# Odd-layer gates as float32r products one block later, and a new order of the routing work at the start of each expert stage

## The chip, the cores and the metric

One NeuronCore of a Trainium2 chip. The metric is device time in microseconds (us) of one execution; it is compared between kernels that run on the same chip. Engines are called PE (TensorE), DVE (VectorE), ACT (ScalarE), POOL (GpSimd) and SP (SyncE, which here only issues the weight loads).

## What is computed

Two residual layers over 512 tokens of width 1024, float32 in and out. Layer 0 has RWKV-7 time mixing and stick-breaking attention, and is not touched by the change. Layer 1 (the odd layer) is a gated recurrence, and both layers end with a mixture of experts. Cut to what matters:

```
# odd layer
u = rmsnorm(x) @ w_in_odd                       # 1024 -> 1280 gate branch | 1280 recurrent branch
rec = causal_depthwise_conv(u[..., 1280:])      # width 4
r = sigmoid(rec_g @ w_rgate[g] + b_rgate)       # 10 blocks g of 128 x 128
i = sigmoid(rec_g @ w_igate[g] + b_igate)
log_a = -8 * r * softplus(-lru_lambda)
h = scan(a = exp(log_a), b = sqrt(1 - a*a) * i * rec)
x = x + (gelu(u[..., :1280]) * h) @ w_out_odd
# every layer
g_idx = argmax(group softmax over 4 groups); top 2 of the group's 4 experts
gates = g_top * e_top / sum(e_top)
y = sum over chosen experts e of gates[e] * ((silu(h @ w_gate[e]) * (h @ w_up[e])) @ w_down[e])
```

## The kernel before, in words

**Precision.** A float32 matrix product is done as three float32r products: each operand is split into a high part (`hi`, an ACT copy that rounds) and a low part (`lo`, a subtraction on DVE or POOL), by `split` (L292), and hi\*hi + hi\*lo + lo\*hi are summed in PSUM. Only small products are left as plain fp32, among them the odd layer's gates (L1035, L1039).

**Order.** The program is written for a planner that orders each engine's instructions by its own cost estimates; `behind(a, b)` (L300) adds an order without a semaphore, so `a` comes after `b` in the planned order. Engines take their instructions in order. `switch` (L394) loads an activation table set and stands behind the activations that are listed for it.

**Odd layer** (`odd`, L994). A loop over 10 blocks g projects a recurrent block (`proj_fm`, L318: 24 products of 512 columns), scales it (L1021, DVE), convolves it (L1031 on ACT, three shifted L1033 on DVE) into `u[:, g]`, and right behind that makes the two gate products in fp32 (L1035, L1039), sigmoid, tanh and sigmoid on ACT (L1036, L1037, L1041), and u\*i on POOL (L1042). Then the table set is switched (L1044), and a second loop projects the 10 gate-branch blocks while decay, square root and scan of the recurrence run beside it (L1047 to L1064). `out_proj` closes the layer.

**Routing.** `route_tile` (L1150) is called per tile of 128 tokens inside `out_proj`. It writes the rows times the norm gain to `HD` in DRAM, from which expert rows are gathered; for the last tile that product is put off (`later`, L1159, on DVE) and called in `moe` as `last_rows` (L1463). `choose` (L1197) picks the experts of a tile. `place` (L1229) counts with triangular products on PE which slot a token has with each expert, and writes the slots (`pm`), the selection for expert 0 (`s0`, L1239) and a column of `rh`. `first` (L1243) forms expert 0's transposed rows with selection products on PE, without a gather.

**Expert stage** (`moe`, L1450). Each expert takes up to 96 tokens. First expert 0's x is split in 8 steps (`cut0`, L1462), then `route` (L1260) computes the gates and, through `slots` (L1308), the row numbers and factors of an expert: `match` (L1254, DVE) compares the slots with `io`, `rows_of` (L1324, PE) multiplies by `rh`, small DVE operations give the index. `fetch` gathers the next expert's rows with an indirect DMA on POOL (L1330). `half` (L1346) is the gate or the up product of an expert, 24 products; `front` the SiLU; `across` (L1334) turns gathered rows; `turn` and `down` are the second product of the expert before; `scatter` adds the result to DRAM. `chunk` (L1427) splits a weight chunk in two halves; for all experts but expert 0 the second halves of chunks 1, 3 and 5 go to POOL. For expert 0 the low parts stand behind `cut0`:

```
            pool = e > 0 and (i, j) in POOL
            if e == 0:
                self.behind(a, self.root)
                if not pool:
                    self.behind(v, self.cut0)
```

Weights come in 1 MB loads on SP's queue, in order, at most five under way (`load`, L1400), into a ring of buffers that `prefetch` (L1414) opens one by one as memory comes free.

## Time and profile before

| | us |
|---|---|
| median of 3 runs | 1229.35 (1228.08 to 1234.36) |
| the profiled execution | 1228.33 |
| its span, first to last instruction | 1226.6 |
| PE busy | 1160.2 |
| DVE busy | 986.5 |
| ACT busy | 807.0 |
| POOL busy | 483.7 |

The span runs through layer 0's mixing (to about 330), its experts (about 378 to 690), the odd layer (about 690 to 905) and its experts (about 910 to the end). How to read it: busy time is how long an engine held an instruction, and matmuls overlap, so PE's busy time is no measure of its speed; the distance between the starts of two matmuls is. The granted clock is the share of full speed (2.4 GHz) that PE had. A gap in brackets in a timeline is idle time of that engine ahead of the row, with what ended it.

### The profile page before, as it was taken

What the parts mean: (1) busy time and instruction counts of PE and PEld (TensorE: products, weight loads), DVE (VectorE), ACT (ScalarE), POOL (GpSimd) and SP (SyncE); (2) the same over time, 40 slices, a digit from 0 to 9 for tenths busy, and PEclk for the clock granted to TensorE, in tenths of its full rate; (3) what the DMA queues carried; (4) which work ended last, traced back from release to release, by engine and by line L of the source; (5) the groups of instructions that cost most, each with busy time, mean ns of one, the idle gap of its engine ahead of it and who ended that gap; (6) DMA issues with size and microseconds to landing.
All of it is one profiled execution on the core that took longest, in us unless ns stands there. A gap on an engine that the chain in (4) does not pass through costs nothing. (4 is left out here: it accounts for less than half of the span.)

```text
span 1226.6 us, 18324 instructions
## 1 busy us (share of the span) xinstructions
PE 1160.2 (95%) x6782; PEld 855.5 (70%) x6783; DVE 986.5 (80%) x1279; ACT 807.0 (66%) x1077; POOL 483.7 (39%) x319
## 2 busy tenths in 40 slices
PE   7999999899997899999999999999988999999997
PEld 6777776776675677777776766777766777777764
DVE  4387796577768799999998565697667999999986
ACT  6533545587536688888887564756436888888883
POOL 9043200210021367667765011300113566666753
PEclk9999999899998999999999999999998999999999
DMA  6312221016867899999993622276578999999974
GB/s 173 86 52 69 69 69 35 2 37 212 297 240 269 293 349 366 358 351 351 350 361 107 187 69 68 70 238 242 203 237 299 349 362 361 352 345 342 349 237 149
DMA packets 152390, 274.47 MB, mean 224 GB/s; under 512 B 8171, under 2 KB 59052, under 8 KB 152294
## 3 DMA queue, kind: packets, MB, share of 16 engines
q1 hardware_dynamic: 142438, 247.85, 58.5%
q0 software_dynamic: 7840, 18.04, 6.3%
q10 hardware_dynamic: 2016, 7.34, 1.5%
q8 instruction: 55, 0.90, 0.3%
q14 instruction: 41, 0.34, 0.1%
HBM read 258.80 MB, written 22.28 MB: 229 GB/s over the span
## 5 line engine op out<-in xcount | busy, mean ns | idle before, releaser
L297 ACT ACTIVATE R<-A 128x1024 fp32r<-128x1024 f32 (+1 forms) x451 | 473.1, 1053 | 193.1 <-PE ps_pj L1353 65.6
L298 DVE TENSOR_TENSOR R<-A,R 128x1024 fp32r<-128x1024 f32 (+1 forms) x362 | 494.1, 1398 | 82.8 <-ACT R L297 78.7
L298 POOL TENSOR_TENSOR R<-A,R 128x1024 fp32r<-128x1024 f32 x89 | 255.1, 2866 | 237.1 <-ACT R L297 232.8
L1354 PE MATMUL ps_pj<-R 128*96 128x512 f32 x512 | 205.6, 402 | 9.9 <-DVE R L298 9.9
L1352 PE MATMUL ps_pj<-R 128*96 128x512 f32 x512 | 206.2, 403 | 0.0
L1353 PE MATMUL ps_pj<-R 128*96 128x512 f32 x512 | 204.1, 399 | 0.0
L327 PE MATMUL ps_pj<-R 128*128 128x512 f32 x296 | 118.3, 400 | 3.5 <-DVE R L298 3.5
L325 PE MATMUL ps_pj<-R 128*128 128x512 f32 x296 | 119.4, 403 | 1.5 <-DVE A L700 0.6
L326 PE MATMUL ps_pj<-R 128*128 128x512 f32 x296 | 119.4, 403 | 0.0
L1354 PEld LDWEIGHTS ps_pj<-R 128*96 128x96 f32 x512 | 84.1, 164 | 47.0 <-DVE R L298 10.9
L1353 PEld LDWEIGHTS ps_pj<-R 128*96 128x96 f32 x512 | 84.4, 165 | 35.5 <-DVE R L298 0.3
L1379 PE MATMUL ps_at<-R 128*96 128x512 f32 x256 | 103.7, 407 | 5.0 <-PEq L1574 1.9
L1352 PEld LDWEIGHTS ps_pj<-R 128*96 128x96 f32 x512 | 84.5, 165 | 33.9 <-issue 0.5
L1381 PE MATMUL ps_at<-R 128*96 128x512 f32 x256 | 101.5, 396 | 0.0
L1380 PE MATMUL ps_at<-R 128*96 128x512 f32 x256 | 101.4, 396 | 0.0
L327 PEld LDWEIGHTS ps_pj<-R 128*128 128x128 f32 x296 | 55.6, 188 | 20.0 <-DVE R L298 5.7
L1388 POOL DMA_INDIRECT YD<-A x30 | 67.3, 2243 | 4.8 <-issue 2.4
L325 PEld LDWEIGHTS ps_pj<-R 128*128 128x128 f32 x296 | 55.6, 188 | 19.2 <-issue 3.4
L1155 POOL TENSOR_TENSOR A<-A 128x1024 f32<-128x1024 f32 x6 | 16.2, 2719 | 126.8 <-DVE A L861 87.2
L326 PEld LDWEIGHTS ps_pj<-R 128*128 128x128 f32 x296 | 55.6, 188 | 14.3 <-issue 3.6
L298 DVE TENSOR_TENSOR R<-ps_rw,R 128x384 fp32r<-128x384 f32 x92 | 47.7, 542 | 12.7 <-ACT R L297 12.6
L1257 DVE TENSOR_TENSOR A<-A 128x384 bf16<-128x384 f32 x32 | 57.8, 1817 | 0.0
(443 smaller groups left out, 1987.0 us busy)
## 6 DMA issues: line engine op xcount, KB each, us to landing
A<-in_exp_w_up_dram SPq DMA_DIRECT2D x61, 1024.0 KB
A<-in_exp_w_down_dram SPq DMA_DIRECT2D x61, 1024.0 KB
A<-in_exp_w_gate_dram SPq DMA_DIRECT2D x59, 1024.0 KB
A<-in_w_in_even_dram SPq DMA_DIRECT2D x27, 512.0 KB
A<-in_w_in_odd_dram SPq DMA_DIRECT2D x20, 512.0 KB
S<-in_exp_w_gate_dram SPq DMA_DIRECT2D x5, 1024.0 KB
A<-in_w_out_odd_dram SPq DMA_DIRECT2D x10, 512.0 KB
A<-in_x_dram SPq DMA_DIRECT2D x8, 512.0 KB
```

The costliest lines, as they stand in the source:

```text
L297: a = self.nc.scalar.activation(hi, src, AF.Copy)
L298: return a, (eng or self.nc.vector).tensor_tensor(lo, src, hi.bitcast(F32), OP.subtract)
L325: nc.tensor.matmul(p[0:n], hi[:, k], Hh[:, k], start=k == 0, stop=False)
L326: nc.tensor.matmul(p[0:n], hi[:, k], Hl[:, k], start=False, stop=False)
L327: nc.tensor.matmul(p[0:n], lo[:, k], Hh[:, k], start=False, stop=k == KD - 1)
L1352: self.nc.tensor.matmul(b, xh[:, k], hi, start=k == 0, stop=False)
L1353: self.nc.tensor.matmul(b, xl[:, k], hi, start=False, stop=False)
L1354: self.nc.tensor.matmul(b, xh[:, k], lo, start=False, stop=k == KD - 1)
L1379: nc.tensor.matmul(yb[n], hh[:, k], hi[:, cs], start=k == 0, stop=False)
L1380: nc.tensor.matmul(yb[n], hl[:, k], hi[:, cs], start=False, stop=False)
L1381: nc.tensor.matmul(yb[n], hh[:, k], lo[:, cs], start=False, stop=k == 3)
L1388: self.nc.gpsimd.indirect_dma_start(out=self.YD[l][:, :], out_offset=bass.IndirectOffsetOnAxis(ap=ix[0:SL], axis=0), in_=y.rearrange("p a ...
```

## The change

1. Odd layer: the two fp32 gate products of a block become three float32r products each. For that `u[:, g]` and the block's gate weights are split. The gates of block g - 1 are made after the projection of block g has closed (`gates`, `self.closed`), those of the last block after the first projection of the gate branch, and the switch of the table set moves there with them.
2. Expert stage: expert 0's chunk 0 is split ahead of the x splits, its low parts behind `chosen` and `placed` instead of `cut0`; the second halves of its chunks 3 and 5 go to POOL. The last tile's row product moves from DVE, behind the x splits, to POOL, once tiles 0 to 2 are placed. `route` first makes what expert 0's SiLU and expert 1's gather need; all that needs the gate values moves into a new function `gates`, called after expert 0's two halves, with the buffers, the load and expert 2's gather that follow from it. `match` reads `io` from a copy in PSUM. Copies of `rh` columns go from DVE to ACT. The count of overflow blocks takes 3 DVE operations instead of 10. Row products are held behind the last product of the half before (`closed`).

The diff, cut to its core:

```diff
@@ odd
+        def gates(g):
+            hi, lo = [self.uq.bufs[g % 2].r(T, off=i * T) for i in range(2)]
+            self.split(hi, lo, u[:, g])
+            wh, wl = [self.wq.r(2, 128, off=i * 256) for i in range(2)]
+            self.split(wh, wl, wgv[:, :, g])
+            z = []
+            for x in range(2):
+                z.append(self.bank("rw"))
+                for i, (a, b) in enumerate(((wh, hi), (wh, lo), (wl, hi))):
+                    m = nc.tensor.matmul(z[x], a[:, x], b, start=not i, stop=i == 2)
+                    if not x and not i:
+                        self.behind(m, self.closed)
...
         for g in range(NB):
             b = self.proj_fm(w, LRU + g * 128, 128, ("pj", "at")[g % 2])
...
-            nc.tensor.matmul(z, wgv[:, 0, g], u[:, g], start=True, stop=True)
...
-            nc.tensor.matmul(z, wgv[:, 1, g], u[:, g], start=True, stop=True)
...
+            if g:
+                gates(g - 1)
...
             scaled(mm[:, g], self.proj_fm(w, g * 128, 128, ("pj", "at")[g % 2]))
+            if not g:
+                gates(NB - 1)
+                self.switch(sig, "exp_and_others")
@@ route_tile
-            self.last_rows = later
...
         if t == NT - 1:
-            self.place(0, t)
+            m = nc.gpsimd.tensor_tensor(h.f(), self.X.f(NT, D)[:, t], self.gn.f(), OP.mult)
+            self.tc.add_manual_dep(m.ins, self.place(0, t).ins.name, mybir.DependencyInfo(
+                mybir.DependencyClass.Sync, mybir.DependencyReason.DATA), reason="order")
+            nc.gpsimd.dma_start(self.HD[t * 128:t * 128 + 128, :], h.f())
...
-            self.sel[0], self.p0 = self.sl.next().b(NT, SL), self.bank("rw")
-            self.match(0)
-            self.rows_of(self.p0[0:SL, 0:3], self.sel[0], self.rh.b(NT, NE, 9)[:, :, 0, 0:3])
@@ match
+        return self.nc.vector.tensor_tensor(self.sel[e], self.pi[:, 256:256 + SL].rearrange("p (a n) -> p a n", a=1).to_broadcast(s),
+                                            self.pm.f(NT, NE)[:, :, e:e + 1].to_broadcast(s), OP.is_equal)
@@ route
-        self.slots(0, 0, 1)
+        nc.scalar.activation(self.pi[:, 256:256 + SL], self.io.f()[:, 0:SL], AF.Copy)
...
-            V.tensor_copy(rh[:, :, :, c], bc(r, NE))
+            nc.scalar.activation(rh[:, :, :, c], bc(r, NE), AF.Copy)
...
+        self.slots(0, 2, 3)
+        self.slots(1, 0, 1)
...
+    def gates(self):
+        self.behind(V.tensor_reduce(gs, gd, AX.X, OP.add), self.lastlo)
...
-            V.tensor_copy(rh[:, :, :, c], ga)
+            nc.scalar.activation(rh[:, :, :, c], ga, AF.Copy)
...
-        self.slots(0, 1, 3)
+        self.slots(0, 0, 2)
+        self.slots(1, 1, 3)
@@ slots
+        self.rows_of(p[:, a * 3:b * 3], self.sel[e], self.rh.b(NT, NE, 9)[:, :, e, a * 3:b * 3], behind=self.closed)
@@ chunk
-            pool = e > 0 and (i, j) in POOL
+            pool = (i, j) in (POOL if e else POOL[1:])
...
-                    self.behind(v, self.cut0)
+                    self.behind(v, self.cut0 if i else self.placed if j else self.chosen)
@@ moe
+        part0 = self.chunk(l, 0, 0)
         for k in range(KD):
             self.cut0 = self.split(nxt[0][:, k], nxt[1][:, k], self.x0[k // 4][:, k % 4 * SL:k % 4 * SL + SL], g=self.gf(l, k))[1]
-        self.last_rows()
...
         self.route(l)
...
-        self.prefetch(l, 1, False)
...
             if e == 0:
-                self.slots(1)
                 fetch(1)
...
-            if e < NE - 2:
+            if 0 < e < NE - 2:
                 self.slots(e + 2)
                 fetch(e + 2)
...
             b = self.half(1, xh, xl, part)
             nc.vector.scalar_tensor_tensor(hd, b, r, hd, OP.mult, OP.mult)
+            if not e:
+                self.gates()
+                yr = Ring(ar, 2, D, *room)
+                self.prefetch(l, 1, False)
+                self.slots(2)
+                fetch(2)
             nxt = turned(e + 1)
```

## Rows read from the trace of the kernel before

**Rows 1.** Windows, steady expert loop: us, busy time (instructions) per engine, clock, DMA share, GB/s.
```profile
590.00:610.00 20.00, 20.00 (x99) 14.23 (x98) 19.94 (x22) 16.65 (x20) 15.54 (x6) 1.00 1.04 359
```

**Rows 2.** Windows, PE behind the first wait of layer 0's experts, columns as above.
```profile
383.50:389.20 5.70, 5.67 (x14) 3.80 (x15) 5.67 (x18) 2.33 (x3) 0.00 (x0) 0.51 0.90 323
```

**Rows 3.** Timeline of PE, start of layer 0's experts.
```profile
377.87 0.46 PE L1352 MATMUL ps_pj<-R 128*96 128x512 f32 x1
...
383.53 0.74 PE L1354 MATMUL ps_pj<-R 128*96 128x512 f32 x1 [4.98 <-DVE R L298]
...
402.00 0.85 PE L1341 MATMUL ps_rw<-A 96*128 96x96 f32 x8 [4.29 <-DMA A<-HD,A]
...
403.15 0.72 PE L1352 MATMUL ps_pj<-R 128*96 128x512 f32 x1
```

**Rows 4.** Timeline of DVE, the same stretch.
```profile
370.02 0.27 DVE L1241 TENSOR_SCALAR A<-A 128x48 bf16<-128x48 f32 x1
...
375.58 0.17 DVE L1237 SCALAR_TENSOR_TENSOR A<-ps_pj,A 128x16 f32<-128x16 f32 x1 [0.92 <-PE ps_pj L1235]
...
380.74 1.22 DVE L1160 TENSOR_TENSOR A<-A 128x1024 f32<-128x1024 f32 x1
```

**Rows 5.** Timeline of PE, start of layer 1's experts.
```profile
910.05 0.45 PE L1352 MATMUL ps_pj<-R 128*96 128x512 f32 x1
...
936.28 0.72 PE L1352 MATMUL ps_pj<-R 128*96 128x512 f32 x1
```

**Rows 6.** Timeline of PE, one block of the odd layer's first loop.
```profile
748.51 1.10 PE L1035 MATMUL ps_rw<-A 128*128 128x512 f32 x2 [0.36 <-DVE A L1033]
...
750.54 0.40 PE L326 MATMUL ps_pj<-R 128*128 128x512 f32 x1
...
755.80 0.39 PE L325 MATMUL ps_at<-R 128*128 128x512 f32 x1
```

**Rows 7.** Timeline of DVE in that loop.
```profile
751.21 0.69 DVE L1021 TENSOR_TENSOR A<-ps_pj,A 128x512 f32<-128x512 f32 x1 [2.84 <-PE ps_pj L327]
...
754.06 2.31 DVE L1033 SCALAR_TENSOR_TENSOR A<-A 128x511 f32<-128x511 f32 x3
...
768.48 3.35 DVE L1033 SCALAR_TENSOR_TENSOR A<-A 128x511 f32<-128x511 f32 x3
```

**Rows 8.** Windows, the odd layer's first loop and the stretch behind it.
```profile
710.50:782.70 72.20, 68.60 (x258) 47.40 (x258) 41.79 (x48) 36.64 (x50) 13.06 (x9) 1.00 0.23 67
785.50:842.00 56.50, 52.89 (x227) 41.86 (x226) 55.89 (x70) 39.41 (x60) 7.31 (x6) 1.00 0.58 190
```

**Rows 9.** Groups of instructions by line and form: busy us, mean ns, idle before.
```profile
L298 DVE TENSOR_TENSOR R<-A,R 128x1024 fp32r<-128x1024 f32 x356 | 488.0, 1404 | 79.7 <-ACT R L297 78.7 <-DMA A<-in_gn_w_dram 0.2
L298 POOL TENSOR_TENSOR R<-A,R 128x1024 fp32r<-128x1024 f32 x89 | 255.1, 2866 | 237.1 <-ACT R L297 232.8 <-DMA A<-in_exp_w_up_dram 3.9
...
L295 ACT ACTIVATE R<-ps_at,A 128x96 fp32r<-128x96 f32 x16 | 4.8, 338 | 4.0 <-PE ps_at L1252 2.6 <-DVE R L296 1.4
...
L830 ACT ACTIVATE R<-A 128x512 fp32r<-128x512 f32 x8 | 4.5, 619 | 0.0
...
L1291 DVE TENSOR_TENSOR A<-A 128x64 f32<-128x64 f32 x4 | 1.1, 277 | 0.1
```

**Rows 10.** All instructions of the match, L1257: duration ns min/median/max.
```profile
L1257 DVE TENSOR_TENSOR A<-A x32: 538/2682/2697, 376.0 to 1123.1; 128x384 bf16<-128x384 f32 x32
```

**Rows 11.** Timeline of POOL, the gather of expert 1 in layer 0.
```profile
394.11 1.19 POOL L1330 DMA_INDIRECT A<-HD,A  x1 [11.28 <-DVE A L1320]
```

**Rows 12.** DMA issues: out<-in, queue, count, KB, median us from issue to landing.
```profile
HD<-A POOLq DMA_DIRECT2D x2, 512.0 KB, 6.9
A<-HD,A POOLq DMA_INDIRECT x30, 7.7
```

**Rows 13.** Timeline of SP, issue of expert 15's gate weights in layer 0.
```profile
618.74 2.97 SPq L1406 DMA_DIRECT2D A<-in_exp_w_gate_dram  x2
```

**Rows 14.** Timeline of PE, first product of expert 15 in layer 0.
```profile
653.97 0.39 PE L1352 MATMUL ps_pj<-R 128*96 128x512 f32 x1
```

More of the change, by code (lines that the diff above doesn't have):

```diff
@@ L41 @@
 WO1 = LOW + 7056
+YR = 17352
 FLY = 5
@@ L1070, in odd @@
             scaled(mm[:, g], self.proj_fm(w, g * 128, 128, ("pj", "at")[g % 2]))
+            if not g:
+                gates(NB - 1)
+                self.switch(sig, "exp_and_others")
+                for x in (self.uq, self.wq):
+                    x.free()
             if g < 2:
@@ L1125, in route_begin @@
         lo = (MID, LOW)[l]
-        self.ss, self.rb, self.s0 = ar.get(16, lo), ar.get(504, lo), ar.get(NT * SL, lo)
+        end = (YR, 1 << 30)[l]
+        self.rb = ar.get(504, MID) if l else ar.take(end, 504)
+        self.ss, self.s0 = ar.get(16, lo, end), ar.get(NT * SL, lo, end)
         self.gn = ar.get(D, lo)
@@ L1281, in route @@
             self.after(nc.scalar.activation(a, a, AF.Exp))
-        V.tensor_reduce(gs, gd, AX.X, OP.add)
+        for b in (self.scr, self.ht, self.ss, self.s0, self.gn):
+            b.free()
+    def gates(self):
+        nc, ar, V, R = self.nc, self.ar, self.nc.vector, self.R
+        bc = lambda a, n: a.to_broadcast([128, NT, n])
+        OH, rh = self.OH.b(NT, NE), self.rh.b(NT, NE, 9)
+        gs, gd, ex, den, g1, EX, ga = [R[k] for k in ("gs", "gd", "ex", "den", "g1", "EX", "ga")]
+        self.behind(V.tensor_reduce(gs, gd, AX.X, OP.add), self.lastlo)
         V.tensor_scalar(den, ex, 1.0, None, OP.add)
@@ L1288, in route @@
         for c in range(3, 6):
[L1289 removed]
+            nc.scalar.activation(rh[:, :, :, c], ga, AF.Copy)
             if c < 5:
                 V.tensor_tensor(ga, ga, rh[:, :, :, c], OP.subtract)
[L1292 to L1294 removed]
+        self.slots(0, 0, 2)
+        self.slots(1, 1, 3)
+        nx, n = self.bank("rw"), (T - 1) // SL
         for t in range(NT):
[L1296 to L1301 removed]
+            m = nc.tensor.matmul(nx[:, 0:16], self.tri[:, 1], OH[:, t], start=t == 0, stop=t == NT - 1)
+            if not t:
+                self.behind(m, self.closed)
+        ex, s = R["n"].rearrange("p t n -> p (t n)"), [128, NE, n]
+        more = R["LG"].rearrange("p t n -> p (t n)")[:, 0:NE * n].rearrange("p (a n) -> p a n", a=NE)
+        V.tensor_tensor(more, nx[:, 0:16].rearrange("p (a n) -> p a n", n=1).to_broadcast(s),
+                        self.io.f()[:, SL - 1:n * SL:SL].rearrange("p (a n) -> p a n", a=1).to_broadcast(s), OP.is_gt)
+        V.tensor_reduce(ex[:, 0:16], more, AX.X, OP.add)
         V.tensor_reduce(ex[:, 16:17], ex[:, 0:16], AX.X, OP.add)
[L1303 removed]
+        self.ext = ar.get(24, 0, self.slots_at[0])
         V.tensor_copy(self.ext.i(17), ex[:, 0:17])
[L1305 removed]
+        for b in (self.rb, self.OH):
             b.free()
@@ L1310, in slots @@
         nc, V = self.nc, self.nc.vector
-        p = self.pi[0:SL, e * 9:e * 9 + 9] if e else self.p0[0:SL, 0:9]
+        p = self.pi[0:SL, e * 9:e * 9 + 9]
         sg = self.sg.f(NE, 3, p=(0, SL))[:, e]
-        if e:
+        if e not in self.sel:
             self.sel[e] = self.sl.next().b(NT, SL)
-            self.match(e)
-        if e or a:
-            self.rows_of(p[:, a * 3:b * 3], self.sel[e], self.rh.b(NT, NE, 9)[:, :, e, a * 3:b * 3])
+            m = self.match(e)
+            if e < 2:
+                self.behind(m, self.placed)
+        self.rows_of(p[:, a * 3:b * 3], self.sel[e], self.rh.b(NT, NE, 9)[:, :, e, a * 3:b * 3], behind=self.closed)
         V.tensor_reduce(sg[:, a:b], p.rearrange("p (c k) -> p c k", c=3)[:, a:b], AX.X, OP.add)
@@ L1322, in slots, with rows_of @@
                 V.tensor_scalar(self.lastt.f(p=(0, SL))[:, 0:1], sg[:, 0:1], self.slot.f()[0:SL, 0:1], 1.0, OP.add, OP.add)
-    def rows_of(self, out, sel, rh, t0=0, t1=NT):
-        for t in range(t0, t1):
-            self.nc.tensor.matmul(out, sel[:, t], rh[:, t], start=t == 0, stop=t == NT - 1)
+    def rows_of(self, out, sel, rh, behind=None):
+        for t in range(NT):
+            m = self.nc.tensor.matmul(out, sel[:, t], rh[:, t], start=t == 0, stop=t == NT - 1)
+            if behind and not t:
+                self.behind(m, behind)
     def gather(self, xg, ix):
@@ L1481, in moe @@
             if e == 0:
-                self.slots(1)
                 fetch(1)
-            part = lambda i, e=e: self.chunk(l, e, i)
+            part = lambda i, e=e: self.chunk(l, e, i) if e or i else part0
             hd = hr.next().f(p=(0, SL))
```

49 lines of the change are left out of this document (17 added, 32 removed).

## The prediction, written before the change was run

> **What bounds the kernel now.** I read the windows of the steady expert loop first [rows 1]: TensorE (PE), VectorE (DVE) and the DMA are all full there. PE decides, since a wait of PE would be listed, and in the loop none is. So time can be won only where PE's own timeline prints an idle gap or where its clock is down, and both stand where the change is made. At the start of layer 0's experts [rows 3] PE issues its first product at 377.87, soon waits 4.98 us for the lower half of a weight, then takes 5.7 us for 14 products (granted clock 0.51, the 1.2 GHz level [rows 2]), and after expert 0 waits 4.29 us for the gathered rows of expert 1. Layer 1 repeats it [rows 5]. In the odd layer [rows 6] the fp32 gate products come behind an idle 0.36 us; from 785 us on DVE is full, 55.9 of 56.5 us [rows 8].
>
> **Part A, the odd layer's gates.** From 710.5 us, where block 2's projection starts, to the end of the gate branch's first projection at 782.7 there are 72.2 us [rows 8]; they hold 9 projections and 10 gate groups. Projection products start 0.229 us apart (23 steps from 750.54 to 755.80 [rows 6]); a projection has 24: 5.49 us. So a gate group costs (72.2 - 49.4)/10 = 2.28 us, and a block 7.77. One group's parts agree: from its start 748.51 to 750.54, where the second projection product behind it starts, less 0.229 for the first one, is 1.8 [rows 6]; the rest is the gap ahead. After the change a group is six one-pass products of 0.229: 1.37 us, a block 6.86. Ceiling 10 x 0.91 = **9.1**.
>
> Added are four splits per block. Of u (512 columns): ScalarE (ACT) 0.62 [rows 9], DVE about 0.69, as its other 512-column operation [rows 7]. Of the gate weights (256 columns): not in the trace; between a 96-column and a 512-column row on ACT, 0.34 to 0.62 [rows 9], between 64 and 512 columns on DVE, 0.28 to 0.69; I take 0.4 each, nearer the small ones in size. DVE's 0.69 + 1.40 + 2.31 = 4.40 per block [rows 7, 9] becomes 5.5, under 6.86: DVE's idle time covers it, and ACT's does (36.6 us busy of 72.2 [rows 8], 10 more). Not surely covered is the chain: u is ready 5.16 us after its projection (751.21 to 754.06 + 2.31 [rows 7]); with split and hand-overs 6.5 us, while the gates come at 6.86. If POOL's product u*i falls on the three shifts, they take 3.35 instead of 2.31 [rows 7]: 7.5. A lateness is halved, as a whole block lies between: block (6.86 + 7.5)/2 = 7.18, 5.9 us won. With one weight split, the next weights' cut and the three gate activations all ahead of it I bound the chain at 10.5: block 8.68, 9.1 us lost. I take **-7.5**, midway between 9.1 and 5.9, as neither the free chain nor the stretched row is nearer.
>
> This arrives: the table switch waits for the last gates, which start at 710.5 + 49.4 + 9 x 1.37 = 772.2 instead of 780, and DVE, full from there to 842 [rows 8], starts that much sooner. What is late next is DVE in that stretch.
>
> **Part B, the start of the experts, in both layers.** From expert 0's first product to expert 1's: 403.15 - 377.87 = 25.3 us [rows 3], in layer 1 936.28 - 910.05 = 26.2 [rows 5]. In it are 48 products (11.0), the transposes of expert 1's rows (1.15, 402.00 to 403.15), the two waits (9.3), and 14 products at the low clock, 14 x (0.405 - 0.229) = 2.5 too long; 1.4 us are left for small row products. So 13.5 us of work: ceilings **11.8** and **12.7**.
> - *First wait.* DVE comes out of the x splits at 380.7 and does the last tile's row product first (1.22 [rows 4]), then the small gate operations among the weight splits. After the change chunk 0 is split while DVE waits for PE (0.92 us idle ahead of the last placing [rows 4], and during the last selection products), and the row product is on POOL. PE goes on from 377.9. Chunk 1 still stands behind the x splits, 380.7 + 1.2 = 381.9; PE is there at 381.1.
> - From there DVE has five weight splits (1.22 alone, as the row product of that size), about 1.4 us of small operations and two matches (0.54 [rows 10]): to 389.3; 10 of PE's products, 2.3 us, follow: 391.6 instead of 388.9. Loss 0 (small ones in gaps) to 2.7; I take 1.7, nearer the full count, DVE being in order. No gap is long, so the full clock is kept.
> - *Second wait.* The gather of expert 1 is issued at 394.11 [rows 11] and used from 402.0; 7.7 us to landing in the median [rows 12]. After: the row product on POOL from the placing of tiles 0 to 2 (370.3 [rows 4]) for 2.9 us, as POOL's other product of that size [rows 9], then the write, 6.9 [rows 12]: 380.1. Gather there, landed at 388; PE wants it at 390. Covered by some 2 us; without that cover PE waits what is missing, up to the old 4.3.
> - *The gates* now stand between expert 0 and 1: eight small DVE operations of at most 0.28 and three ACT copies of some 0.34 [rows 9], 3.3 us in a row beside PE's last 2.3. PE's row products queue behind them, and expert 1's transposes behind those if so planned: 0 to 2 us; I take 0.8, since only the excess of 1.0 is uncovered.
> - *At the front* splitting chunk 0 can delay the placing: 0 to 1.2; casts that leave DVE give back up to 0.28 each, as the 64-column row [rows 9]. I take 0.2.
>
> Per layer 2.7 of the ceiling is lost: **-9.1** and **-10.0**.
>
> **Costed at nothing.** ACT's copy of io and the casts: ACT waits for PE there. POOL's splits of expert 0 (2.87 each [rows 9]): the second gather stands behind the first of them, but has an expert's time to land. The load moved behind the gates, and every load queued behind it on SP: expert 15's gate weights are issued at 618.74 and used from 653.97, 35 us later [rows 13, 14]; this cover, less five transfers under way, goes if PE gains much more than 12 us. The shorter match (median 2.68 now [rows 10]) pays nothing: PE never waits for it in the loop.
>
> **Sum**, against the profiled execution: 1228.3 (span 1226.6 + 1.7) - 7.5 - 9.1 - 10.0 = 1201.7; the median shown is 1.0 above that execution. Forecast **1202**, own range 1194 to 1209.
>
> **Rivals.** About 0.5% (6 us) is what a measurement of this kernel can tell from no change.
> 1. *DVE paces expert 0.* Beside a POOL split DVE's two-input operations stretch (match 0.54 to 2.68 [rows 10]): five splits at the mean 1.40 instead of 1.22, one block of 2.1, and PE's gaps bring the low clock back (2.5): 5.5 us per layer, **1213**. For: DVE has little room there. Against: POOL takes only one split ahead of PE's last product. Chance 0.15. The Trainium skill, page "SBUF — State Buffer", section "Who interferes with whom", speaks for this rival: a DVE instruction with two SBUF inputs and a GpSimd instruction that reads SBUF exclude each other for a whole instruction. By it alone POOL's row product and two splits could hold DVE 3 x 2.9 us per layer, and the sum would be 1219; the spread of the match agrees with it. By the same rule a match that reads io from PSUM no longer waits.
> 2. *The gates wait in every block.* u ready at 8.3 us (shifts stretched, one ACT operation more): block 7.58, part A gives 1.9: **1207**. For: the 3.35 row; against: 5.16 in the old order. 0.09.
> 3. *It does not do what it says.* A stated order is only a lower bound: the planner can still put chunk 0 behind the x splits, and POOL's queue can hold the gather. Part B then gives 2 us per layer, part A little: **1222 to 1226**. 0.08.
> 4. *Slower.* The row products of expert e+2 are held behind the last product of expert e's gate half, in PE's queue. If the match, on the full DVE, is later than that, PE waits at 13 places per layer: at 2.1 us each 55 us, **1256**; slower than now by 0.5% from 1.3 us each on. For: DVE is full [rows 1]. Against: nothing in the loop waits now. 0.06.
>
> **Numbers.** Forecast 0.62, rivals 0.15, 0.09, 0.08, 0.06. Faster 0.86 (forecast, 1 and 2), same 0.08, slower 0.06. The range 1192 to 1217 takes in the bounds of the sum and rivals 1 and 2.
>
> **What would show it.** Right: gate groups of six products, 1.4 us; blocks of 6.9 to 7.2; the table switch 7 to 8 us earlier; no wait of 5 us behind expert 0's first products and no low clock there; the gather of expert 1 issued 2 to 4 us after expert 0's first product; expert 1 some 16 us behind expert 0. Wrong: an idle gap ahead of each gate group, a clock near 0.5 in expert 0, a wait for gathered rows, or PE waits in the loop.

## The result, and the profile of the changed kernel

The changed kernel takes 1218.44 us in the median (1213.68 to 1219.83, five runs), the kernel before 1229.26 (1228.08 to 1234.36, five runs): a ratio of 0.9896 (95% interval 0.9876 to 0.9915). It is faster, by 10.8 us (about 1%) instead of the 27 forecast, and lies above both ranges of the prediction, which end at 1209 and 1217. In one run each of `odd_alone` and `rows_last` below (1338.8 and 1628.2 us) the mean granted clock was only 0.81 and 0.65, and medians and ratios leave them out. The changed kernel's profiled execution took 1217.41 us with a span of 1215.7; the span before was 1226.6.

Where the 10.9 us between the two profiled spans lie, from PE's timelines:

| stretch | before | after | difference | forecast |
|---|---|---|---|---|
| start to expert 0's first product, layer 0 | 377.87 | 379.61 | +1.7 | 0 |
| from there to expert 2's first product, layer 0 | 44.13 | 40.86 | -3.3 | -9.1 |
| on to the odd layer's first projection | 272.66 | 272.73 | +0.1 | 0 |
| odd layer, first projection to first placing | 205.8 | 201.05 | -4.7 | -7.5 |
| on to expert 0's first product, layer 1 | 9.62 | 9.05 | -0.6 | 0 |
| from there to expert 2's first product, layer 1 | 44.70 | 41.53 | -3.2 | -10.0 |
| on to the end | 271.85 | 270.87 | -1.0 | 0 |

The first line is no cost of the change: in two executions of the same code up to that product it starts at 377.87 (before) and at 381.03 (the run `odd_alone` below).

**The expert stage.** PE's timeline at the start of layer 0's experts, where [rows 3] had waits of 4.98 and 4.29 us:

```profile
379.61 0.47 PE L1384 MATMUL ps_pj<-R 128*96 128x512 f32 x1
...
392.90 0.47 PE L1386 MATMUL ps_pj<-R 128*96 128x512 f32 x1 [1.19 <-POOL R L299]
...
396.79 1.54 PE L1373 MATMUL ps_rw<-A 96*128 96x96 f32 x8 [2.63 <-DMA A<-HD,A]
...
398.68 0.72 PE L1384 MATMUL ps_pj<-R 128*96 128x512 f32 x1
...
400.23 0.41 PE L1356 MATMUL ps_o<-A 128*96 128x6 bf16 x4 [0.82 <-ACT A L1315]
```

The first wait is gone. In its place PE waits for a split on POOL, for expert 1's gathered rows, and inside expert 1 for the copies of the gate values. Expert 1 starts 19.1 us behind expert 0 (forecast: 16). POOL's timeline says why:

```profile
375.07 0.57 POOL L1194 DMA_DIRECT2D HD<-A  x1 [0.30 <-POOL A L1191]
...
383.95 6.48 POOL L1362 DMA_INDIRECT A<-HD,A  x1 [8.30 <-DVE A L1294]
390.46 2.38 POOL L299 TENSOR_TENSOR R<-A,R 128x1024 fp32r<-128x1024 f32 x1
```

The gather holds POOL for 6.48 us, not for the 1.19 of [rows 11], and the split stands behind it. Its rows land at 396.75, 12.8 us after it is issued. On DVE the index (L1350) is ready only at 383.66, and then a train of five splits runs without a gap; the gather ends 1.0 us after that train:

```profile
383.45 0.21 DVE L1350 TENSOR_SCALAR A<-A 96x1 int32<-96x1 f32 x1
...
383.71 5.76 DVE L299 TENSOR_TENSOR R<-A,R 128x1024 fp32r<-128x1024 f32 x5
...
390.07 2.87 DVE L1313 TENSOR_TENSOR A<-A 128x64 f32<-128x64 f32 x1
```

The third row is one of the small gate operations (0.22 us in index_first below): beside POOL's late split, 390.46 to 392.84, it takes 2.87. So POOL waits for DVE in the gather, and DVE for POOL right behind it. The gather of [rows 11] had subtractions of the same kind beside it in the kernel before, but a small reduction of data in PSUM stood between two of them; the gather, issued at 394.11, ended at 395.30, beside the second subtraction:

```profile
394.31 0.16 DVE L1318 TENSOR_REDUCE A<-ps_o 96x3 f32<-96x9 f32 x1
394.39 1.22 DVE L298 TENSOR_TENSOR R<-A,R 128x1024 fp32r<-128x1024 f32 x1
```

Layer 1 repeats what the changed kernel does in layer 0 (gather 6.17 us, gate operation 3.09), and expert 2's rows come late there too:

```profile
903.30 0.47 PE L1384 MATMUL ps_pj<-R 128*96 128x512 f32 x1
...
921.97 0.72 PE L1384 MATMUL ps_pj<-R 128*96 128x512 f32 x1
...
938.60 0.85 PE L1373 MATMUL ps_rw<-A 96*128 96x96 f32 x8 [1.37 <-DMA A<-HD,A]
```

The windows (columns as in [rows 1]) show the clock behind the waits: 0.54, near the 1.2 GHz level, from expert 1's transposes on. It falls in the wait for the gathered rows (0.69 from 393.90 to 396.79) and is at 0.50 from its end on, ahead of the wait for the gate values; the second row shows that. The third row is the whole stretch from expert 0's first product to expert 2's.

```profile
396.80:406.00 9.20, 8.38 (x38) 6.22 (x39) 5.96 (x14) 4.04 (x8) 2.88 (x2) 0.54 0.56 196
...
396.79:398.68 1.89, 1.89 (x12) 1.89 (x13) 0.43 (x1) 0.80 (x2) 0.00 (x0) 0.50 1.03 342
...
379.61:420.47 40.86, 35.81 (x171) 24.35 (x169) 35.57 (x64) 28.44 (x44) 20.51 (x7) 0.87 0.89 316
```

The same stretch of the kernel before:

```profile
377.87:422.00 44.13, 34.87 (x161) 24.35 (x159) 36.38 (x74) 27.29 (x39) 9.43 (x6) 0.88 0.81 282
```

**The odd layer.** Blocks are 7.33 us long (752.57 to 759.90; from 737.56 on 7.31 to 7.58), against 7.46 to 8.01 before. PE issues a group's first product and then waits for the lower half of u:

```profile
752.57 0.39 PE L1035 MATMUL ps_rw<-S 128*128 128x512 f32 x1
753.19 1.43 PE L1035 MATMUL ps_rw<-S 128*128 128x512 f32 x5 [0.23 <-DVE S L299]
...
759.90 0.40 PE L1035 MATMUL ps_rw<-S 128*128 128x512 f32 x1
```

ACT's and DVE's timelines of that block hold the chain. ACT takes the sigmoid of the block before (L1038, which waits for PE's gate product) ahead of this block's convolution (L1052):

```profile
753.96 0.69 ACT L1038 ACTIVATE A<-ps_rw,A 128x512 f32<-128x512 f32 x1 [0.36 <-PE ps_rw L1035]
754.54 0.81 ACT L1052 ACTIVATE A<-A 128x512 f32<-128x512 f32 x1
...
759.11 0.63 ACT L298 ACTIVATE S<-A 128x512 fp32r<-128x512 f32 x1 [2.27 <-DVE A L1054]
```

The shifts (L1054) follow on DVE, with the split of the gate weights between them at 1.48 us (beside POOL's u\*i), then the split of u (ACT, 759.11), then the next gate product:

```profile
755.38 1.53 DVE L1054 SCALAR_TENSOR_TENSOR A<-A 128x511 f32<-128x511 f32 x2 [0.52 <-ACT A L1052]
756.87 1.48 DVE L299 TENSOR_TENSOR S<-A,S 128x256 fp32r<-128x256 f32 x1
758.28 0.74 DVE L1054 SCALAR_TENSOR_TENSOR A<-A 128x509 f32<-128x509 f32 x1
```

So the block time is a loop: gate product, sigmoid, convolution, shifts, split of u, gate product.

**The match** in its new form, all instructions (columns as [rows 10]), is never stretched any more:

```profile
L1271 DVE TENSOR_TENSOR A<-ps_o,A x32: 539/540/551, 379.3 to 1130.5; 128x384 bf16<-128x384 f32 x32
```

### The profile page after: what moved, and what is told of

It reads as the page before. It is cut to its first block, busy times and chain, and to the rows that moved or that the text cites. A ratio compares the mean times of both kernels' runs of the same rounds, so it can differ in the third digit from the quotient of the medians.

```text
span 1215.7 us, 18409 instructions
## 1 busy us (share of the span) xinstructions
PE 1157.6 (95%) x6810; PEld 856.7 (70%) x6811; DVE 962.0 (79%) x1269; ACT 818.7 (67%) x1111; POOL 492.0 (40%) x325
## 5 line engine op out<-in xcount | busy, mean ns | idle before, releaser
L299 DVE TENSOR_TENSOR R<-A,R 128x1024 fp32r<-128x1024 f32 x358 | 486.7, 1391 | 107.5 <-ACT R L298 102.4
L299 POOL TENSOR_TENSOR R<-A,R 128x1024 fp32r<-128x1024 f32 x93 | 230.1, 2475 | 263.7 <-ACT R L298 262.0
L1386 PEld LDWEIGHTS ps_pj<-R 128*96 128x96 f32 x512 | 83.1, 162 | 40.5 <-POOL R L299 3.5
L1385 PEld LDWEIGHTS ps_pj<-R 128*96 128x96 f32 x512 | 83.6, 163 | 35.6 <-DVE R L297 1.1
L1384 PEld LDWEIGHTS ps_pj<-R 128*96 128x96 f32 x512 | 83.5, 163 | 33.5 <-ACT R L298 0.9
L1362 POOL DMA_INDIRECT A<-HD,A x30 | 64.6, 2154 | 22.1 <-DVE A L1294 11.7
L1175 POOL TENSOR_TENSOR A<-A 128x1024 f32<-128x1024 f32 x6 | 16.2, 2718 | 132.0 <-DVE A L862 92.4
L328 PEld LDWEIGHTS ps_pj<-R 128*128 128x128 f32 x296 | 55.6, 188 | 19.1 <-DVE R L299 5.6
L1412 PEld LDWEIGHTS ps_at<-R 128*96 128x96 f32 x256 | 41.5, 163 | 21.2 <-ACTq L1613 3.7
```

Of the source, the lines that this page charges most:

```text
L299: return a, (eng or self.nc.vector).tensor_tensor(lo, src, hi.bitcast(F32), OP.subtract)
L328: self.closed = nc.tensor.matmul(p[0:n], lo[:, k], Hh[:, k], start=False, stop=k == KD - 1)
L1384: self.nc.tensor.matmul(b, xh[:, k], hi, start=k == 0, stop=False)
L1385: self.nc.tensor.matmul(b, xl[:, k], hi, start=False, stop=False)
L1386: m = self.nc.tensor.matmul(b, xh[:, k], lo, start=False, stop=k == KD - 1)
L1412: nc.tensor.matmul(yb[n], hh[:, k], hi[:, cs], start=k == 0, stop=False)
```

## The experiments

All are changes of the changed kernel, except the first. "To expert 1" and "to expert 2" are us from expert 0's first product to that expert's, in layer 0 / layer 1. Ratios are to the kernel before on the same chip, with 95% intervals.

| kernel | median us | ratio | to expert 1 | to expert 2 |
|---|---|---|---|---|
| before | 1229.3 | | 25.3 / 26.2 | 44.1 / 44.7 |
| changed | 1218.4 | 0.9896 (0.9876 to 0.9915) | 19.1 / 18.7 | 40.9 / 41.5 |
| odd_alone | 1225.3 | 0.9965 (0.9952 to 0.9979) | 26.1 / 25.4 | 44.2 / 44.6 |
| conv_first | 1212.4 | 0.9863 (0.9846 to 0.9879) | 20.0 / 18.6 | 42.2 / 40.3 |
| hi_for_lo | 1213.6, one run | | 15.5 / 15.5 | 37.8 / 40.0 |
| one_input | 1214.6, one run | | 16.2 / 16.2 | 39.9 / 40.8 |
| index_first | 1212.6 | 0.9875 (0.9842 to 0.9908) | 15.8 / 15.7 | 38.4 / 38.8 |
| late_gates | 1207.9 | 0.9828 (0.9812 to 0.9844) | 14.3 / 14.3 | 37.2 / 36.6 |
| early_across | 1213.1 | 0.9864 (0.9848 to 0.9880) | 13.6 / 13.5 | 40.4 / 39.8 |
| all_orders | 1209.0 | 0.9834 (0.9821 to 0.9848) | 13.5 / 13.5 | 39.1 / 39.0 |
| rows_last | 1211.8 | 0.9863 (0.9834 to 0.9892) | 14.3 / 14.3 | 41.5 / 35.9 |
| rows_last_early | 1207.7 | 0.9823 (0.9801 to 0.9845) | 13.5 / 13.5 | 36.9 / 38.5 |
| late_hi | 1211.8, one run | | 14.9 / 14.8 | 37.7 / 38.7 |
| late_conv | 1205.4 | 0.9802 (0.9784 to 0.9820) | 14.3 / 14.3 | 37.2 / 38.1 |

The two last columns are of one execution each. Kernels with the same code in these stretches differ there by up to 1.5 us (late_gates and late_conv: 36.6 and 38.1 in layer 1; changed and conv_first: 40.9 and 42.2 in layer 0), so a smaller difference in one stretch shows nothing by itself. The intervals of conv_first and index_first overlap that of the changed kernel; what they win is read from the stretches and the waits in them.

**odd_alone: the odd layer's part by itself.** The edit is the diff's part for `odd` on the kernel before, nothing else.

> The kernel before with the odd layer's gates of the change and nothing else of it. The two traces give 4.7 us to the odd layer (from its first projection to the last placing: 198.9 us instead of 203.7, less what the start of it shifted). Theory (the two parts do not touch each other): 4 to 5 us faster than before, near 1224.5, blocks of 7.3 us. Rival (part of the odd layer's gain belongs to the loads or memory that the expert stage's change moves): 2 us or less, or blocks of another length.

The odd layer takes 200.7 us (698.6 to 899.3), 205.8 before and 201.05 in the changed kernel; the lengths in the expectation are some 2 us too short on both sides, their difference holds. Blocks are 7.35 us:

```profile
750.38 0.41 PE L1034 MATMUL ps_rw<-S 128*128 128x512 f32 x1
...
757.73 0.39 PE L1034 MATMUL ps_rw<-S 128*128 128x512 f32 x1
```

The interval (2.6 to 5.9 us) holds the 4.7, and the expert stages are as long as before. Within that interval the parts do not touch each other, and the rest of the gain is the expert stage's.

**conv_first: one order added in the odd layer.**

```diff
-            nc.scalar.activation(u[:, g], b, AF.Identity, ...)
+            conv = nc.scalar.activation(u[:, g], b, AF.Identity, ...)
...
                 gates(g - 1)
+                self.behind(sig[-3], conv)
```

> One order added in the odd layer: ACT takes the convolution's first operation of block g ahead of the sigmoid of block g - 1's gates. Theory (the block's 7.33 us are a loop: gate product, sigmoid, convolution behind it on ACT, shifts on DVE, split of u, gate product): the loop is cut, PE waits no more for the lower half of u, a block takes 6.9 us, and the end of the odd layer is 3 to 4 us sooner, near 1214.5. Rival (the split of u is late for DVE's stretched operations beside POOL's u*i, whatever ACT's order): blocks stay at 7.2 to 7.4 us, and the time is that of the changed kernel within 1 us. Second rival (block time falls, but the stretch behind it, where DVE is full, ends no sooner): blocks of 6.9 us and less than 1 us won.

PE's gate groups come without a wait, 6.91 us apart:

```profile
751.44 1.64 PE L1035 MATMUL ps_rw<-S 128*128 128x512 f32 x6
...
758.35 1.55 PE L1035 MATMUL ps_rw<-S 128*128 128x512 f32 x6
```

The convolution is now the earlier one on ACT, 0.94 us after the gate group's start instead of 1.97:

```profile
752.38 0.81 ACT L1052 ACTIVATE A<-A 128x512 f32<-128x512 f32 x1
753.09 0.67 ACT L1038 ACTIVATE A<-ps_rw,A 128x512 f32<-128x512 f32 x1
```

DVE is stretched as before, only elsewhere: the planner moved the weights' split behind the shifts (0.42 us there), and the three shifts take 3.40 beside POOL's u\*i instead of 2.31 [rows 7]:

```profile
753.65 3.40 DVE L1054 SCALAR_TENSOR_TENSOR A<-A 128x511 f32<-128x511 f32 x3
```

So the first rival falls: the stretch stays and the block is at the 6.86 of the forecast. The odd layer takes 198.0 us (693.28 to 891.3), 7.8 less than before; the table switch starts at 775.00, 8.1 us earlier than before, of which 1.4 are the layer's earlier start (forecast: 7 to 8; in the changed kernel 777.99, 5.2 earlier). The second rival falls too.

**hi_for_lo and one_input: what holds the gather.** In the first, DVE's five lower halves of expert 0's chunks 1 to 3 are left out; in the second they are replaced:

```diff
+            if e == 0 and 0 < i < 4 and not pool:
+                self.behind(self.nc.scalar.activation(hi, src, AF.Copy), self.root)
+                parts += [(hi[:, n], hi[:, n]) for n in range(h)]
+                continue
```

```diff
+            if e == 0 and 0 < i < 4 and not pool:
+                a = self.nc.scalar.activation(hi, src, AF.Copy)
+                v = self.nc.vector.tensor_scalar(lo, src, 0.0, None, OP.mult)
```

> Left out: the lower halves that DVE makes for expert 0's chunks 1 to 3 (five per layer); PE multiplies by the upper half in their place, so the products stay as many. Theory (the gather of expert 1 on POOL is held off by DVE's train of five subtractions, 5.76 us): with the train gone the gather takes 1.0 to 2.0 us on POOL instead of 6.48 and 6.17, POOL's split comes in time (no wait of 1.2 to 1.4 us of PE for it), and the rows land 8 to 9 us after the gather's start, so that PE's wait of 2.6 us for them is 0 to 0.5. Rival (the gather is slow by itself there, for the write of the rows before it or for the weight loads in the DMA engines): it stays at 5 to 6.5 us and lands 12 to 13 us after its start.

> Left out: the same five lower halves per layer; DVE writes zero times the weight in their place, an operation of the same size that reads one operand instead of two. If what holds the gather off is that DVE reads two operands from SBUF, the gather takes 1.0 to 2.5 us on POOL though DVE's train is still there; if any run of DVE operations of this size holds it off, the gather ends with the train, as in the changed kernel (6.5 us, or as long as the train then lasts).

Without the train the gather takes 1.07 us on POOL, and the rows are no longer waited for; PE's wait for POOL's split stays (1.34), against the expectation. It has another cause here: POOL is idle for 5 us ahead of that split, which starts at 390.36, right behind ACT's copy of the same half (389.23 to 390.28); the planner put that copy behind the SiLU and its table load.

```profile
384.29 1.07 POOL L1362 DMA_INDIRECT A<-HD,A  x1 [8.31 <-PE ps_pj L1385]
```

With one-input operations the train is 3.10 us long and the gather takes 3.99; the rows are still waited for (2.44):

```profile
381.58 3.99 POOL L1362 DMA_INDIRECT A<-HD,A  x1 [8.31 <-DVE A L1294]
```

```profile
381.34 3.10 DVE L1473 TENSOR_SCALAR R<-A 128x1024 fp32r<-128x1024 f32 x5
```

In both kernels with a train the gather ends about 1 us after it (390.43 against 389.47, 385.57 against 384.44). So the train holds it, the rival of slow loads or a slow write falls, and two operands are not what it takes: the other branch of the second expectation holds.

**index_first: the fix of one line.**

```diff
-        self.slots(0, 2, 3)
         self.slots(1, 0, 1)
+        self.slots(0, 2, 3)
```

> One line moved: the row numbers of expert 1 are worked out ahead of expert 0's own factor, so that the gather is issued some 2.5 us sooner, before DVE's train of splits begins. Theory (held off by the train, and late by 4 us in its index): the gather is issued about 1.7 us after expert 0's first product instead of 4.3, takes 1 to 2 us on POOL, and lands before PE wants the rows; PE's waits of 1.2 and 2.6 us behind expert 0 go and with them most of the low clock in expert 1. I expect 4 us per layer (2.5 to 5.5): 8 us under the changed kernel, near 1210. Rival (slow for the write ahead of it or the loads): it is issued sooner, takes 6 us all the same, and the gain is 2.5 us per layer at most, 1213 to 1218. Rival (the gates' row products are the next wait): PE waits 2 to 3 us for them inside expert 1, and the gain is 1 to 2 us per layer.

The gather starts 1.95 us after expert 0's first product (381.23), ahead of the train, and is short:

```profile
383.18 1.07 POOL L1362 DMA_INDIRECT A<-HD,A  x1 [5.90 <-DVE A L1350]
```

PE takes expert 1's transposes without a wait, and expert 1 starts 15.8 us behind expert 0, as forecast for the change itself (16). But inside expert 1 the wait for the gate copies grows:

```profile
394.33 0.86 PE L1373 MATMUL ps_rw<-A 96*128 96x96 f32 x8
...
396.99 0.48 PE L1384 MATMUL ps_pj<-R 128*96 128x512 f32 x1 [0.36 <-ACT R L298]
...
398.68 0.41 PE L1356 MATMUL ps_o<-A 128*96 128x6 bf16 x4 [1.21 <-ACT A L1315]
```

and the clock behind it is still down (0.58). Here it is this wait that the fall goes with: the clock is 1.00 up to 396.90 and 0.50 from 398.68.

```profile
394.30:396.90 2.60, 1.44 (x17) 1.07 (x16) 2.60 (x5) 2.60 (x6) 0.00 (x0) 1.00 1.06 388
...
397.00:405.00 8.00, 6.79 (x26) 4.56 (x27) 6.92 (x17) 3.70 (x7) 3.43 (x2) 0.58 0.84 290
```

So to expert 2 it wins 2.5 and 2.7 us per layer, not 4: theory and last rival share it.

**late_gates: the gate values after expert 1's first half.** On index_first:

```diff
+            if e == 1:
+                self.gates()
+                yr = Ring(ar, 2, D, *room)
+                self.prefetch(l, 1, False)
             if 0 < e < NE - 2:
...
             if not e:
-                self.gates()
-                yr = Ring(ar, 2, D, *room)
-                self.prefetch(l, 1, False)
-                self.slots(2)
+                self.slots(2, 0, 1)
+                self.slots(2, 2, 3)
```

with `slots(1, 2, 3)` in `route`, `slots(1, 1, 2)` and `slots(2, 1, 2)` in `gates`, a third selection buffer, and expert 1's transposes held behind expert 0's last product.

> On top of the index of expert 1 first: the gate values are worked out after expert 1's first half instead of between expert 0 and 1; expert 1's factor and expert 2's index go ahead of them, with a third selection buffer. Theory (after the gather, the gates' chain over ACT and DVE is the next wait, and with the idle of 3.6 us around it brings the low clock to 14 products): the wait of 1.2 us for the gate copies inside expert 1 goes, and expert 2's rows come in time in layer 1 (1.6 us there). From expert 0's first product to the first product of its second matrix (32.8 and 33.2 us with the index first): 29 to 31.5; 2 to 4 us per layer, 1205 to 1209. Rival (the low clock comes from the idle time ahead of expert 1's first product, for the turned rows and their split, and stays): 1 to 1.5 us per layer, 1209.5 to 1210.5.

The clock is full over the whole stretch (1.00, column 7), and expert 2's rows come in time:

```profile
377.63:414.79 37.16, 33.62 (x182) 22.48 (x181) 35.71 (x67) 28.05 (x44) 15.01 (x7) 1.00 0.98 349
```

It wins 1.2 and 2.2 us more per layer, and 4.7 by the medians, as expected. The waits did not go, against the theory; they moved to later products of expert 1:

```profile
402.29 0.30 PE L1358 MATMUL ps_o<-A 128*96 128x6 bf16 x4 [1.02 <-ACT A L1316]
...
404.44 0.30 PE L1358 MATMUL ps_o<-A 128*96 128x3 bf16 x4 [1.08 <-DVE A L1350]
```

**early_across, all_orders: expert 1's transposes ahead of expert 0's end.** all_orders has conv_first as well. On late_gates:

```diff
+                if hook and k == 6:
+                    self.closed = m
+                    hook()
...
-            b = self.half(1, xh, xl, part)
+            b = self.half(1, xh, xl, part, None if e else lambda: x1.append(turned(1)))
```

> On top of the late gates: the transposes of expert 1's rows go between the last but two and the last two groups of products of expert 0 (6 products ahead of its end), so that their split on ACT and DVE lies beside products. Theory: PE goes from expert 0 to expert 1 without the idle 1.3 to 2.5 us, the clock stays full in expert 1, and expert 0's first product to the first product of its second matrix takes 28 us or a little less (72 products of 0.229 us are 16.5, turning and small products 2.5, chunk waits the rest): together with the late gates 4 to 5 us per layer, 1203 to 1205. Rival (the rows land only after that place): PE waits for the gather again, 1 to 3 us, with nothing won over the late gates, or a loss.

> The early transposes together with the convolution ahead of the sigmoid in the odd layer. If the two stretches do not touch each other, the odd layer's 3 to 6 us come on top: 1198 to 1201, about what was forecast for the change. Rival: what one stretch wins the other loses (loads of weights arrive no sooner), 1203 or more.

Expert 1 starts after 13.6 us instead of 14.3, with no wait for the rows, but more than that is lost to the gate values, PE standing 3.65 us for them inside expert 1:

```profile
390.07 0.45 PE L1391 MATMUL ps_pj<-R 128*96 128x512 f32 x1
...
404.37 0.41 PE L1358 MATMUL ps_o<-A 128*96 128x6 bf16 x4 [3.65 <-ACT A L1316]
```

ACT's copy waits for a gate operation on DVE. It takes 2.39 us, beside POOL's split of 398.23 to 401.68, and 0.22 in late_gates; weight splits stand between the gate operations ahead of it:

```profile
399.38 2.39 DVE L1314 TENSOR_TENSOR A<-A 128x64 f32<-128x64 f32 x1
```

Both expectations miss; only the odd layer's share in all_orders (4.1 us by the medians) came as expected.

**rows_last, rows_last_early: the gate values' row products behind expert 1.** The calls leave `gates` and expert 1's first half; the second kernel has the early transposes and conv_first too. On late_gates:

```diff
             b = self.half(1, xh, xl, part)
...
+            if e == 1:
+                self.slots(0, 0, 2)
+                self.slots(1, 1, 2)
+                self.slots(2, 1, 2)
+                self.slots(3)
+                fetch(3)
```

> On top of the late gates: the row products that carry the gate values (experts 0, 1 and 2) and the index of expert 3 come behind the last product of expert 1 instead of inside it, beside the second product of expert 0. Theory (what PE waits for inside expert 1 is this chain, 1.0 and 1.1 us in layer 0, 1.0 and 0.5 in layer 1): both waits go, expert 0's first product to the first product of its second matrix takes 29 to 30 us instead of 31.6 and 31.0, 1203 to 1206. Rival (DVE is the bound there: 30.7 us busy of the 31.6 with the late gates): other waits of PE, for splits on DVE, take their place, and the time stays within 1 us of 1207.9.

> The same with the transposes of expert 1's rows 6 products ahead of expert 0's end, and the convolution ahead of the sigmoid in the odd layer. Theory (in the run with early transposes the gain of 2.4 us up to expert 1's first product was lost to the wait of 3.65 us for the gate values, and the low clock behind it): without that wait the stretch takes 26 to 29 us, and with 3 to 4 us of the odd layer the time is 1194 to 1201. Rival (DVE is the bound): the stretch takes 30 to 31 us, PE waits for DVE's splits, and the time is 1202 to 1205, the odd layer's gain alone.

The second matrix of expert 0 starts after 28.5 us in both layers, as the theory has it, but the wait then stands inside it, 3.70 us in layer 0 and 1.01 in layer 1:

```profile
405.38 0.45 PE L1412 MATMUL ps_at<-R 128*96 128x512 f32 x1
...
410.46 0.41 PE L1354 MATMUL ps_o<-A 128*96 128x3 bf16 x4 [3.70 <-DVE A L1346]
```

What PE waits for in layer 0 is a reduction on DVE (410.26) that stands behind weight splits; the last of them takes 3.38 us, from 406.30, beside POOL's split of 405.81 to 408.59.

So rows_last is slower than late_gates, and rows_last_early no faster though it has the odd layer's share: the theory holds up to the second matrix and falls behind it. The 2.4 us that its expectation gives to the early transposes are a misreading: the product after 12.0 us is one of expert 0's last six, and the early transposes win 0.7 to 0.8. Wherever PE's queue holds these row products in these kernels, it stands for them (0.5 to 3.7 us).

**late_hi: is DVE the bound now?** It is late_gates without the five lower halves of hi_for_lo (left out again).

> The late gates with the five lower halves per layer left out that DVE makes for expert 0's chunks 1 to 3 (PE multiplies by the upper half in their place): 5.8 us of DVE's work less, the same PE order. Theory (with the late gates DVE is the bound from expert 0's first product to expert 2's: 35.7 and 35.1 us busy of 37.2 and 36.6): the stretch falls to 32.5 to 35 us, PE's waits for the gate values (about 1 us each) shrink or go. Rival (the bound is the chain of gathers, small products and gate values, whatever DVE's load): it stays at 36 to 37.5 us with DVE idle for 5 us and more.

The theory fails: the stretch is no shorter, 37.7 and 38.7 us, at the rival's figure or above it.

```profile
379.18:416.88 37.70, 33.35 (x182) 22.54 (x181) 30.07 (x62) 27.94 (x44) 14.22 (x7) 1.00 0.97 344
```

PE still waits 1.03 and 1.07 us for the same copies and row products. But the 5.6 us that DVE has less to do in layer 0 lie ahead of expert 1's first product. From there to the end of the first of these waits DVE is busy 10.18 of 10.35 us in both kernels. The first two rows are late_gates, the last two late_hi, cut at expert 1's first product:

```profile
377.63:391.94 14.31, 13.72 (x75) 8.90 (x73) 13.82 (x28) 12.17 (x23) 4.25 (x2) 1.00 1.04 381
391.94:402.29 10.35, 8.47 (x43) 5.39 (x44) 10.18 (x19) 7.07 (x11) 5.13 (x3) 1.00 1.02 372
...
379.18:394.04 14.86, 13.49 (x74) 8.98 (x72) 8.21 (x24) 12.05 (x23) 3.46 (x2) 1.00 1.04 386
394.04:404.39 10.35, 8.44 (x42) 5.39 (x43) 10.18 (x18) 7.07 (x11) 5.11 (x3) 1.00 1.02 362
```

One wait is new: as in hi_for_lo, PE stands 1.13 us for POOL's split, which it does not in late_gates. So the run shows that DVE's load ahead of expert 1 is not the bound. Whether its load inside expert 1 is, it does not show.

**late_conv: the two fixes that worked, together.** late_gates and conv_first.

> The late gates (transposes of expert 1 behind expert 0, gate values behind expert 1's first half) together with the convolution ahead of the sigmoid in the odd layer. Theory: the two lie in different stretches and add up: 1207.9 less 3 to 6 us, 1202 to 1205, expert stages of 37 us up to expert 2 as with the late gates and odd blocks of 6.9 us. Rival (what is won in the odd layer is given back at the start of layer 1's experts, where the weight loads then come too late): 1206 to 1208, with waits of PE for a load there.

It is the fastest version of the study: 24.5 us under the kernel before on the same chip, and 13 under the changed one by the medians. The odd layer takes 198.0 us (689.79 to 887.8). Layer 1's stretch is 1.5 us longer than in late_gates, with the same waits (0.99 and 0.54 for the row products) and no wait for a load; what differs is the clock, 0.96 in column 7:

```profile
896.74:934.85 38.11, 35.12 (x182) 23.38 (x181) 35.11 (x66) 27.90 (x43) 15.77 (x8) 0.96 0.92 327
```

That execution is the slowest of the five (1208.62; the others 1203.75 to 1206.32), and 1.5 us is how far two executions of one stretch differ above. So neither the rival's loss nor its waits for a load are shown.

## Why the prediction was wrong, step by step

The sign was right, the size was not: 10.8 us of 27. Layer 0's stretch from expert 0's to expert 2's first product, taken apart from PE's timeline (products: 120 at 0.23 us; waits: the printed gaps; low clock: what products more than 0.36 us apart without a gap take too long; rest: transposes, small products and gaps too short to be printed):

| us | before | changed | index_first | late_gates |
|---|---|---|---|---|
| products | 27.6 | 27.6 | 27.6 | 27.6 |
| waits | 9.3 | 5.0 | 2.8 | 3.5 |
| low clock | 4.0 | 2.5 | 3.0 | 0.4 |
| rest | 3.2 | 5.8 | 4.9 | 5.7 |
| sum | 44.1 | 40.9 | 38.4 | 37.2 |

- **First wait (forecast: gone, 1.7 us lost to DVE).** Right, and better: only 0.36 us of PE's waits in expert 0 are for DVE, and no low clock comes of it.
- **Second wait (forecast: gather at 380.1, landed at 388, covered by some 2 us).** This is the step that failed. It followed the row write and not the index: that stood behind expert 0's factor and the x splits on DVE and came at 383.66. And it took 7.7 us from issue to landing, the median of gathers that hold POOL for about 1 us; beside the train of five splits this one held POOL for 6.48 and landed after 12.8, at 396.75. That cost 2.63 us at the rows and 1.19 at POOL's split, which had been costed at nothing, and the low clock in expert 1. hi_for_lo and one_input show the hold, index_first the remedy: its gather lands after 7.4 us, and PE waits neither for the rows nor for POOL's split. The write itself, taken at 6.9 us, never mattered.
- **Gates between expert 0 and 1 (forecast 0.8).** A wait of 0.82 is there, but that it has the forecast's size is luck. It was sized as the part of a chain of small operations that PE's last products of expert 0 do not cover; what PE waits for, inside expert 1, is ACT's third copy, which stands in ACT's queue behind the split of the late rows, and ahead of which a gate operation on DVE had been held for 2.87 us by POOL's split. The clock is low behind it for some ten products, but it was already at 0.50 ahead of it, from the wait for the rows on. Index_first, which does not wait for rows, does show the clock falling with the wait for the gate values (1.21). Before the change the clock had been low in expert 1 too (4.0 us in all, of which the 2.5 in expert 0 were counted). The ceiling ended at expert 1's first product, while the moved work was paid behind it: 6.2 us are won up to there and 2.9 lost by expert 2.
- **Small products.** They were taken to stay the same; with row products in more groups (171 PE instructions instead of 161 in the stretch) the rest grows by 2.6 us. Some of it is the low clock once more (eight transposes take 1.54 us at 396.79, 0.85 before); how much is the products and how much short gaps is not settled.
- **Layer 1** repeats this: 3.2 us instead of 10.0, with one more wait of 1.37 for expert 2's rows, whose index came at the end of the gate operations.
- **Part A (forecast 7.5).** The terms were right: six products of 1.4 us, block 6.86, a chain on u as the risk. Wrong is "a lateness is halved, as a whole block lies between": ACT's order closes the chain within a block, so the block is as long as the loop, 7.33 us. conv_first cuts it and gives 7.8 us. That this is near the 7.5 is luck, since 7.5 was a midpoint between the free chain's 9.1 and the stretched one's 5.9. So a step that depends on an engine's queue order was costed without that order.
- **Rivals.** The one that DVE paces expert 0 gave 1213, a time not far off, but PE's waits for DVE in expert 0 are 0.36 us and not the 5.5 per layer it named. The Trainium skill, page "SBUF — State Buffer", section "Who interferes with whom", was cited for it. The exclusion shows both ways, elsewhere than the rival had it: POOL's gather waits for DVE's train, and a gate operation of DVE for POOL's split. The rival that POOL's queue can hold the gather had the right place and 2 us per layer for part B, where 3.3 and 3.2 came, but DVE's train held the gather and not POOL's queue. The blocks of 7.33 us lie between the 7.18 of the stretched forecast and the 7.58 of the second rival. The slower case is not there: from expert 2 to expert 15 layer 0 takes 231.94 us, 231.97 before.

Why the stretch ends at 37 us and not at the 35 of the forecast stays open. late_hi rules out DVE's load ahead of expert 1 alone. What is left is the gate values' chain, hopping between the in-order queues of DVE and ACT, on a DVE that is full inside expert 1 and that POOL's splits hold: 2.39 us ahead of the wait of 3.65 in early_across, 3.38 ahead of the 3.70 in rows_last, and in late_gates 2.24 for an operation on 10 columns (L1009) shortly ahead of the wait of 1.08 in layer 0, which is 0.53 in layer 1, where that operation is not. This is argued from the timelines; no run takes POOL's splits, or the chain, out of that place.

## What to carry to other kernels

When work is moved out of a wait, follow it to the next point where the old and the new order agree again, and count the clock and the waits up to there, not up to the end of the gap. A gather issued by POOL has a price that depends on what DVE runs beside it (1.07 to 6.48 us here): read its duration from a row with the same neighbours, and put its index ahead of the long train on the other engine. The same holds for a small DVE operation beside a long one on POOL. Where a chain passes an in-order queue twice, write down that queue's order; one instruction in the wrong place makes the chain a loop.

## What the runs showed of the hardware that was not expected

- **A gather on POOL ends with DVE's train.** It takes 1.07 us with DVE idle or on operands from PSUM (hi_for_lo, index_first), 6.48 beside 5.76 us of two-operand subtractions, and 3.99 beside 3.10 us of one-operand multiplications, each time to about 1 us after the train. In the kernel before, where a reduction of PSUM data parts two subtractions, it takes 1.19. The Trainium skill's page above says that DVE's two-input operations contend with GpSimd instructions that read SBUF, and reports that such an operation did not stall a DMA issued from GpSimd. The first agrees with a gather that has its index in SBUF. The second agrees with the plain row write of the kernel before, which takes 0.57 us on POOL beside such a subtraction (both from 382.26); the gather of the changed kernel differs, and the measurement decides. That a one-operand operation on SBUF data can hold it off too is what the same section says of the two-port modes; the trace agrees (3.99 us).
- **POOL's splits hold DVE, down to its smallest operations.** Beside one of some 2.4 us on POOL, a DVE operation on two operands of 64 columns takes 2.87 (changed) and 2.39 (early_across) instead of 0.22, and one on a single operand of 10 columns 2.24 (late_gates) instead of 0.16 (early_across).
- **The match got shorter and the gathers longer.** Reading `io` from PSUM the match takes 0.54 us instead of a median of 2.68 [rows 10], but the gathers of the loop take 1.79 us in the median, where they took 0.98 before. That the one follows from the other is not shown. PE sees neither.
- **The row write lands in 3.6 us** in the median here, 6.9 before [rows 12], by POOL's queue both times.
- **The same waits do not always bring the low clock**: layer 1's stretch has a granted clock of 1.00 in late_gates and 0.96 in late_conv, with waits of the same length.
